# Staggered start addresses in SBUF for the operands of a hybrid attention and retention layer

## The chip, the cores and the metric

The kernel runs on one NeuronCore of a Trainium2 chip. The metric is device time in microseconds. Before the change the median of three runs is 953.46 us (952.16 to 954.02). The profiled execution shown below took 951.88 us, of which 950.1 us lie between its first and its last instruction.

## The reference

One encoder layer over x of 512 rows and 2,048 columns, in float32, then a final RMSNorm:

```
mod = silu(c) @ w_ada + b_ada;  shift, scale, gate = split(mod, 3)
h    = rms_norm(x, g) * (1 + scale) + shift
proj = h @ w_in                                # 512 x 2048 times 2048 x 7168
q_a, k_a, v_a, z_a, q_r, k_r, v_r, z_r = split(proj)
y_a  = dilated window attention, 8 heads of 128: three patterns mixed by their log-sum-exp
y_r  = retention, 4 heads (qk 128, v 256), forward and backward, normalised per head
y    = concat(y_a * silu(z_a), y_r * silu(z_r))
out  = rms_norm(x + gate * (y @ w_out), final_gain)
```

## The kernel before

TensorE multiplies float32 data in its reduced form (float32r). To keep float32 accuracy each operand is split in a high part, which is the value rounded to that form, and a low part, which is what the rounding left. A product is then three matmuls, high times high (line 90) and the two mixed ones (line 92), all added up in one PSUM bank:

```
def mm3(o, lh, ll, rh, rl, start, stop, swap=False):
    nc.tensor.matmul(o, lh, rh, start=start, stop=False, skip_group_check=True)
    for a, b in ((ll, rh), (lh, rl)) if swap else ((lh, rl), (ll, rh)):
        nc.tensor.matmul(o, a, b, ...)
```

The first operand of a matmul is the stationary one, 128 x 128, which a weight load brings into the array; the second is the moving one, 256 or 512 columns. In the profile's rows "pp<-wlo,hh" the moving operand stands first.

**Tiles.** h is held transposed, as 16 tiles hh0 to hh15 of its high parts (line 98), each 128 partitions by 512 floats, and as low parts hl in six groups (line 200). A row of 512 floats is 2,048 bytes in a partition. Weights come from HBM into tiles called raw (line 78), 1,024 floats long. conv (line 167) turns 512 of them into a pair: ScalarE copies to whi (line 174), VectorE subtracts to get wlo (line 179). There are three buffers of each. In the first part a unit of 256 columns of the projection has either "T" form, where weights are stationary and h moves with 512 columns, or "N" form, where h is stationary and 256 columns of weights move (line 647).

**Stages.** The prelude (lines 95 to 477) loads x and c, turns x with TensorE and makes the shift and scale of the first row block; its pools xp, x3p and aap are given back when it is done. While x is turned, a few matmuls of constant tiles, ident and ones, are issued to keep TensorE going (warm, line 399). Then h is made in chunks of 1, 2, 2, 3, 4 and 4 row blocks, and for every chunk the first 13 projection units (of 28) get their share of products; VectorE adds these up in SBUF (acc, line 955; in the rows, "pw" is the bank of such a share and "pp" the bank of a whole unit). The other units run over all 16 blocks at once (whole, line 1058). Attention heads (line 743) and retention heads (line 806) are cut in pieces that stand in a queue, and after every block of matmuls one group of pieces is taken from it (run_queue, line 591). Matmuls of attention and retention show as sp, tp and op.

**Output projection.** y is split like h: yh and yl, 16 tiles each, from pool opA (lines 1163 to 1171), in the place that h had. Three passes take 512, 512 and 512 columns with weights moving ("po", whi and wlo; line 1123), a fourth takes 256, and the last 256 columns are split earlier and kept in tiles lhi and llo of pool yp (line 1270). finish (line 1216) adds the residual and takes squares, and store (line 1241) scales and writes out.

**Order.** Everything is issued in the order of the Python code; in the prelude pin keeps that order. Loads run ahead of their conversion by LEAD or LEAD1 items and conversions ahead of their matmuls by LOOK items (feed, line 600). Nearly all loads are issued by SyncE's queue.

**Pools.** const (line 56) holds constants to the end: among them c_row (line 95), bg_row (line 112), ones (line 138) and row0 (line 314). wp holds raw, whi and wlo. hp holds hh and hl. The left pools are stacked from low addresses up, hp and opA from the high end down.

Of the kernel before, what the change touches and what calls it, by code (L numbers as in the profile page):

```python
# [9 lines left out]
F32 = mybir.dt.float32  # L10
F32R = mybir.dt.float32r
# [6 lines left out]
P = 128  # L18
D = 2048
S = 512  # L20
NT = S // P
NK = D // P
# [18 lines left out]
FIRST_W = OFF_KA + UC  # L41
LAG = 3
RAW, RAW1, WB, LOOK, LEAD, LEAD1, EB, YB = 3, 3, 3, 2, 4, 8, 1, 22
GR = 2
GATE_RATE = 0.9
N_FIRST = 13
# [4 lines left out]
def trunk_kernel(ctx, tc, x, c, norm_gain, w_ada, b_ada, w_in, w_out, dec_f, dec_b, final_gain, out):  # L51
    nc = tc.nc
# [3 lines left out]
    const = ctx.enter_context(tc.tile_pool(name="const", bufs=1))  # L56
    wp = ctx.enter_context(tc.tile_pool(name="wp", bufs=2))
# [5 lines left out]
    def bank(pool, nm):  # L63
        return pool.tile([P, 512], F32, tag="b", name=nm)
# [7 lines left out]
    def f32(ap):  # L72
        return ap.bitcast(F32)
# [18 lines left out]
            nc.tensor.matmul(o, a, b, start=False, stop=stop and b is (rl if swap else rh), skip_group_check=True)  # L92


    c_row = const.tile([NK, P], F32, name="c_row")
    hp_scope = ExitStack()
    hp = hp_scope.enter_context(tc.tile_pool(name="hp", bufs=1, side="right"))
    hh = [hp.tile([P, S], F32R, name=f"hh{k}") for k in range(NK)]

    groups = [range(sum(CHUNKS[:i]), sum(CHUNKS[: i + 1])) for i in range(len(CHUNKS))]  # L100
    xt_tiles = {i: hp.tile([P, len(g), S], F32, tag=f"g{i}", name=f"xT{i}") for i, g in enumerate(groups) if i}
# [6 lines left out]
    xp = x_scope.enter_context(tc.tile_pool(name="xp", bufs=1, side="right"))  # L108

    bg_row = const.tile([48, P], F32, name="bg_row")
    raw0 = [xp.tile([P, NK, P], F32, name=f"raw0{b}") for b in range(2)]
    xn = [(x3p if t == 3 else xp).tile([P, D], F32, name=f"xt{t}") for t in range(NT)]

# [19 lines left out]

    ident = const.tile([P, P], F32, name="ident")
    make_identity(nc, ident)
    ones = const.tile([P, P], F32, name="ones")
    nc.gpsimd.memset(ones, 1.0)
    ones_r = const.tile([P, 1], F32R, name="ones_r")  # L140
    mhalf = const.tile([P, 4], F32, name="mhalf")
# [14 lines left out]
    pin = tc.keep_in_program_order  # L156
    marks = {}

    def after(ins, ref):
        tc.add_manual_dep(  # L160
            ins.ins,
            ref.ins.name,
            mybir.DependencyInfo(mybir.DependencyClass.NoSync, mybir.DependencyReason.DATA),
            reason="after",
        )

    def conv(src, n, pin_low=None):
        hi = wp.tile([P, 512], F32R, tag="whi", name="whi", bufs=WB)
        lo = wp.tile([P, 512], F32R, tag="wlo", name="wlo", bufs=WB)
        dh, dl = hi[:, :n], lo[:, :n]  # L170
        if len(src.shape) == 3:
            dh = dh.rearrange("p (k f) -> p k f", k=src.shape[1])
            dl = dl.rearrange("p (k f) -> p k f", k=src.shape[1])
        c1 = nc.scalar.copy(dh, src)  # L174
        if pin_low is not None:
            pin_low.append(lambda: pin(nc.vector.tensor_tensor(dl, src, f32(dh), op=ALU.subtract)))
            pin(c1)
            return hi, lo
        c2 = nc.vector.tensor_tensor(dl, src, f32(dh), op=ALU.subtract)  # L179
        marks["conv"] = marks.get("conv", 0) + 1  # L180
        if marks["conv"] < 3:
            after(c1, marks["hh"])
            after(c2, marks["hl"])
        return hi, lo
# [126 lines left out]
    psk3 = bank(psM, "psk3")  # L311


    row0 = const.tile([1, 2 * P], F32, name="row0")

    def sums0(b, i):
        for a in range(8 * i, 8 * i + 8):
# [80 lines left out]

    def warm(n, ps):
        for _ in range(n):  # L400
            pin(nc.tensor.matmul(ps[:, 128:256], ones, ident, start=True, stop=True))

    A, B = slice(0, 3 * P), slice(3 * P, S)
    warm(WARM[0], psk3)
    squares_a(0)
    squares(0)
# [3 lines left out]
    scaled(0, P, 1024)  # L410
    silu_c()
    warm(WARM[1], psk3)
    k0_part(0)
    turned(0, 0)
# [6 lines left out]
    for t in (1, 2):  # L421
        squares_a(t)
        squares(t)
        factor(t)
    warm(WARM[2], psk3)
    turn_rows()
    sums0(0, 0)
# [18 lines left out]
    sums0_turned()  # L446
    pinned = []
    first_w = conv(raw_w[:, : 2 * UC], 2 * UC, pinned)
    shift_scale0()
    turned(1, 2)  # L450
# [108 lines left out]
    def shared_conv(c0s, k0, nk):  # L559
# [16 lines left out]
        def cv(j):  # L576
            off = (c0s[j] - lo_c) // UC
            if nk == 1:
                if k0 == 0 and lo_c == FIRST_W:
                    st[0] = first_w  # L580
                if off // 2 not in st:
                    a, b = off // 2 * 512, min(off // 2 * 512 + 512, m * UC)
                    st[off // 2] = conv(st["raw"][:, 0, a:b], b - a)
                w = st[off // 2]
                o = off % 2 * UC
                return w[0][:, o : o + UC], w[1][:, o : o + UC]
            return conv(st["raw"][:, :, off * UC : (off + 1) * UC], nk * UC)
# [336 lines left out]
    for ci, nk in enumerate(CHUNKS):  # L924
# [18 lines left out]
        for u in order:  # L943
# [22 lines left out]
            if u < N_PERSIST:  # L966
                pss = lambda u=u: persist[u]
                start, stop = ci == 0, lastc
            elif u in kept:
                pss = lambda u=u, kept=kept: kept[u]  # L970
                start, stop = False, u not in keep_now
            else:
                pss = lambda: [bank(psA, "pw") for _ in range(2)]
                start, stop = True, u not in keep_now
# [19 lines left out]
    def gate_pieces(h):  # L994
        st = {}
        gs = slice(2 * D + h * 512, 2 * D + (h + 1) * 512)

        def load(kr):
            raws[h * NK + kr] = pools["w"].tile([P, 512], F32, tag="graw", name="graw", bufs=GR)
            nc.sync.dma_start(raws[h * NK + kr], wa[kr * P : (kr + 1) * P, gs])  # L1000

        def add(kr):
            raw = raws[h * NK + kr]
            if kr == 0:
                st["acc"] = pools["w"].tile([P, 512], F32, tag="gacc", name="gacc", bufs=1)
                nc.vector.tensor_scalar_mul(st["acc"], raw, ct[:, 0:1])
            else:
                nc.vector.scalar_tensor_tensor(  # L1008
                    st["acc"], raw, ct[:, kr : kr + 1], st["acc"], op0=ALU.mult, op1=ALU.add
                )  # L1010

        def parts():
            st["parts"] = conv(st["acc"], 512)

        def total():
            row = pools["w"].tile([1, 512], F32, tag="grow", name="grow", bufs=1)
            nc.sync.dma_start(row, b_ada[0:1, gs])
            ps = bank4("psg")[0:1, :]
            for i in range(2):
                nc.tensor.matmul(ps, ones_r, st["parts"][i], start=i == 0, stop=i == 1)  # L1020
            nc.vector.tensor_tensor(row, row, ps, op=ALU.add)
            nc.sync.dma_start(grow_d[0:1, h * 512 : (h + 1) * 512], row)

        return load, add, parts, total
# [6 lines left out]
    gp = [gate_pieces(h) for h in range(4)]  # L1031
    for n in range(4 * NK + GR):

        def step(n=n):
            if n >= GR:
                gp[(n - GR) // NK][1]((n - GR) % NK)
            if n < 4 * NK:
                gp[n // NK][0](n % NK)

        gate.append(step)  # L1040
        if n >= GR and (n - GR) % NK == NK - 1:
            gate.extend([None, gp[(n - GR) // NK][2], gp[(n - GR) // NK][3]])
    gcount = [0]
# [114 lines left out]
    yh, yl = [y0[:, 0:S].bitcast(F32R)], [y0[:, S : 2 * S].bitcast(F32R)]  # L1158
# [3 lines left out]

    opA = ctx.enter_context(tc.tile_pool(name="opA", bufs=1, side="right"))
    for k in range(NK):
        hi = opA.tile([P, S], F32R, name=f"yh{k}")
        lo = opA.tile([P, S], F32R, name=f"yl{k}")
        if k:
            yh.append(hi)
            yl.append(lo)
        else:  # L1170
            y0 = hi, lo
# [135 lines left out]
    for t in range(NT):  # L1307
        ts = slice(t * P, (t + 1) * P)
        ps = bank(psP, "po")[:, :256]
# [30 lines left out]
```

## Time and profile before

| what | value |
|---|---|
| runs, median (lowest to highest) | 953.46 us (952.16 to 954.02) |
| profiled execution, its span | 951.88 us, 950.1 us |
| granted TensorE clock, mean | 0.997 |
| instructions of TensorE | 5,602 matmuls, 5,602 weight loads |
| moved by DMA | 141.50 MB, 149 GB/s on average |

A row of a table of groups gives the source line, engine, operation, tile written and tiles read, shapes and count; then the busy time in us and the mean duration of one in ns; then the idle time of the engine just before these instructions and what ended it. A row of the timeline gives start and length in us, engine, line, operation and tiles. Successive matmuls overlap in time, so the distance between the starts of two of them is shorter than the duration of one.

### The profile page before, as it was taken

What the parts mean: (1) busy time and instruction counts of PE and PEld (TensorE: products, weight loads), DVE (VectorE), ACT (ScalarE), POOL (GpSimd) and SP (SyncE); (2) the same over time, 40 slices, a digit from 0 to 9 for tenths busy, and PEclk for the clock granted to TensorE, in tenths of its full rate; (3) what the DMA queues carried; (4) which work ended last, traced back from release to release, by engine and by line L of the source; (5) the groups of instructions that cost most, each with busy time, mean ns of one, the idle gap of its engine ahead of it and who ended that gap; (6) DMA issues with size and microseconds to landing.
All of it is one profiled execution on the core that took longest, in us unless ns stands there. A gap on an engine that the chain in (4) does not pass through costs nothing.

```text
span 950.1 us, 14445 instructions
## 1 busy us (share of the span) xinstructions
PE 928.7 (98%) x5602; PEld 812.3 (85%) x5602; DVE 619.6 (65%) x1096; ACT 379.0 (40%) x747; POOL 12.5 (1%) x25
## 2 busy tenths in 40 slices
PE   7899999999999999999999999999999999999996
PEld 5787788888888888988998899998899978888896
DVE  4899999959787876765456555746734283455543
ACT  4842425252254655544344232432333362333321
POOL 1000000000000000000000000000000000000000
PEclk9999999999999999999999999999999999999998
DMA  9997898533642222212225616436322267334304
GB/s 328 337 310 244 267 327 292 163 94 121 206 149 70 87 67 67 63 50 89 68 67 178 199 45 211 127 98 209 112 67 90 67 199 257 98 111 133 111 1 178
DMA packets 110244, 141.50 MB, mean 149 GB/s; under 512 B 5800, under 2 KB 81496, under 8 KB 109792
## 3 DMA queue, kind: packets, MB, share of 16 engines
q1 hardware_dynamic: 109072, 137.27, 45.0%
q10 hardware_dynamic: 1008, 3.28, 0.9%
q8 instruction: 44, 0.72, 0.3%
q14 instruction: 24, 0.20, 0.1%
q0 software_dynamic: 96, 0.03, 0.0%
HBM read 136.36 MB, written 4.20 MB: 148 GB/s over the span
## 4 chain that ended last, share of the span: by engine, by line
PE 81%; DVE 6%; DMA 6%; ACT 2%; issue 2%; SPq 1%; POOL 0%; POOLq 0%; DVEq 0%; ACTq 0%
PE pp L92 23%; PE po L92 12%; PE pp L90 12%; PE pw L92 12%; PE po L90 6%; PE pw L90 6%; PE op L92 3%; DMA graw<-in_w_ada_dram 2%; DMA araw<-in_w_ada_dram 2%; PE sp L92 2%; PE op L90 2%; PE tp L783 1%; DVE wlo L179 1%; DVE aacc L235 1%; SPq L117 1%
## 5 line engine op out<-in xcount | busy, mean ns | idle before, releaser
L174 ACT CAST whi<-raw 128x512 fp32r<-128x512 f32 (+1 forms) x289 | 174.8, 606 | 402.6 <-PE pp L92 186.5
L179 DVE TENSOR_TENSOR wlo<-raw,whi 128x512 fp32r<-128x512 f32 (+1 forms) x288 | 193.0, 671 | 185.4 <-ACT whi L174 181.1
L92 PE MATMUL pp<-wlo,hh 128*128 128x256 f32 x576 | 160.4, 278 | 0.5 <-DVE wlo L179 0.5
L90 PE MATMUL pp<-whi,hh 128*128 128x256 f32 x576 | 160.8, 279 | 0.0
L92 PE MATMUL pp<-whi,hl 128*128 128x256 f32 x576 | 160.1, 278 | 0.0
L92 PEld LDWEIGHTS pp<-wlo,hh 128*128 128x128 f32 x576 | 108.2, 188 | 1.6 <-DVE wlo L179 0.7
L90 PEld LDWEIGHTS pp<-whi,hh 128*128 128x128 f32 x576 | 108.3, 188 | 1.1 <-issue 0.2
L92 PEld LDWEIGHTS pp<-whi,hl 128*128 128x128 f32 x576 | 108.7, 189 | 0.0
L90 PE MATMUL pw<-hh,whi 128*128 128x512 f32 x256 | 102.4, 400 | 4.7 <-ACT acc L953 2.6
L90 PE MATMUL pp<-hh,whi 128*128 128x512 f32 x256 | 101.0, 394 | 0.4 <-DVE kl L683 0.4
L92 PE MATMUL pw<-hh,wlo 128*128 128x512 f32 x256 | 100.7, 394 | 0.1
L92 PE MATMUL pp<-hl,whi 128*128 128x512 f32 x256 | 100.8, 394 | 0.0
L92 PE MATMUL pp<-hh,wlo 128*128 128x512 f32 x256 | 100.7, 395 | 0.0
L92 PE MATMUL pw<-hl,whi 128*128 128x512 f32 x256 | 100.2, 391 | 0.0
L92 PE MATMUL po<-wlo,yh 128*128 128x512 f32 (+1 forms) x252 | 92.5, 367 | 0.0
L92 PE MATMUL po<-whi,yl 128*128 128x512 f32 (+1 forms) x252 | 92.4, 367 | 0.0
L90 PE MATMUL po<-whi,yh 128*128 128x512 f32 (+1 forms) x252 | 92.4, 367 | 0.0
L235 DVE SCALAR_TENSOR_TENSOR aacc<-araw,ct,aacc 128x512 f32<-128x512 f32 (+2 forms) x75 | 76.0, 1013 | 5.5 <-ACT aacc L231 4.3
L955 DVE TENSOR_TENSOR acc<-acc,pw 128x512 f32<-128x512 f32 x100 | 66.8, 682 | 7.3 <-PE pw L92 7.1
L1008 DVE SCALAR_TENSOR_TENSOR gacc<-graw,ct,gacc 128x512 f32<-128x512 f32 x60 | 44.9, 749 | 39.2 <-DMA graw<-in_w_ada_dram 38.5
L90 PEld LDWEIGHTS pw<-hh,whi 128*128 128x128 f32 x256 | 48.1, 188 | 20.0 <-DVE acc L955 5.7
L90 PEld LDWEIGHTS pp<-hh,whi 128*128 128x128 f32 x256 | 48.2, 188 | 11.2 <-DVE kl L683 0.9
(241 smaller groups left out, 1565.1 us busy)
## 6 DMA issues: line engine op xcount, KB each, us to landing
raw<-in_w_in_dram SPq DMA_DIRECT2D x94, 512.0 KB, 3.8
araw<-in_w_ada_dram SPq DMA_DIRECT2D x48, 512.0 KB, 5.8
graw<-in_w_ada_dram SPq DMA_DIRECT2D x64, 256.0 KB, 3.0
raw<-in_w_out_dram SPq DMA_DIRECT2D x32, 512.0 KB, 4.0
raw<-in_w_in_dram SPq DMA_DIRECT2D x16, 384.0 KB, 5.1
araw<-in_w_ada_dram SPq DMA_DIRECT2D x16, 384.0 KB, 4.9
res<-in_x_dram SPq DMA_DIRECT2D x16, 256.0 KB, 6.5
raw<-in_w_in_dram SPq DMA_DIRECT2D x11, 256.0 KB, 5.8
```

Source lines behind the costliest of these rows:

```text
L90: nc.tensor.matmul(o, lh, rh, start=start, stop=False, skip_group_check=True)
L92: nc.tensor.matmul(o, a, b, start=False, stop=stop and b is (rl if swap else rh), skip_group_check=True)
L117: q.dma_start(raw0[b][:, i * 8 : (i + 1) * 8], wa[i * 8 * P : (i + 1) * 8 * P, b * D : b * D + P].rearrange("(a p) f -> p a f", p=P),)
L174: c1 = nc.scalar.copy(dh, src)
L179: c2 = nc.vector.tensor_tensor(dl, src, f32(dh), op=ALU.subtract)
L235: ins = nc.vector.scalar_tensor_tensor(acc[:, :, :n], rv[:, a], ct[:, kr + a : kr + a + 1], acc[:, :, :n], op0=ALU.mult, op1=ALU.add,)
L783: nc.tensor.transpose(tp_[:, j * P : (j + 1) * P], pt[:, j * P : (j + 1) * P], ident)
L955: nc.vector.tensor_tensor(accs[u][i], accs[u][i], ps[i], op=ALU.add)
L1008: nc.vector.scalar_tensor_tensor(st["acc"], raw, ct[:, kr : kr + 1], st["acc"], op0=ALU.mult, op1=ALU.add)
```

## The change

Tiles of hh and of yh get 24 floats (PAD) more than they use, so that the next tile begins 2,144 bytes on instead of 2,048; within its tile the data begin at float 0 for k = 0 to 3 and 8 to 11 and at float 4 for the others. whi and wlo get the same PAD; whi begins at float 0 and wlo at float 4. The low parts hl and yl stay as they are. To make room, c_row, bg_row and row0 are allocated from the prelude's pool xp instead of const, and ones has one column instead of 128; the warm-up matmuls take ident as stationary operand in place of ones.

```diff
+PAD = 24
-    c_row = const.tile([NK, P], F32, name="c_row")
+    def stagger(k):
+        return k // 4 % 2 * 4
...
-    hh = [hp.tile([P, S], F32R, name=f"hh{k}") for k in range(NK)]
+    hh = [hp.tile([P, S + PAD], F32R, name=f"hh{k}")[:, stagger(k) : stagger(k) + S] for k in range(NK)]
...
-    bg_row = const.tile([48, P], F32, name="bg_row")
+    c_row = xp.tile([NK, P], F32, name="c_row")
+    bg_row = xp.tile([48, P], F32, name="bg_row")
...
-    ones = const.tile([P, P], F32, name="ones")
+    ones = const.tile([P, 1], F32, name="ones")
...
-        hi = wp.tile([P, 512], F32R, tag="whi", name="whi", bufs=WB)
-        lo = wp.tile([P, 512], F32R, tag="wlo", name="wlo", bufs=WB)
+        hi = wp.tile([P, 512 + PAD], F32R, tag="whi", name="whi", bufs=WB)[:, 0:512]
+        lo = wp.tile([P, 512 + PAD], F32R, tag="wlo", name="wlo", bufs=WB)[:, 4:516]
...
-    row0 = const.tile([1, 2 * P], F32, name="row0")
+    row0 = xp.tile([1, 2 * P], F32, name="row0")
...
-            pin(nc.tensor.matmul(ps[:, 128:256], ones, ident, start=True, stop=True))
+            pin(nc.tensor.matmul(ps[:, 128:256], ident, ident, start=True, stop=True))
...
-        hi = opA.tile([P, S], F32R, name=f"yh{k}")
+        hi = opA.tile([P, S + PAD], F32R, name=f"yh{k}")[:, stagger(k) : stagger(k) + S]
         lo = opA.tile([P, S], F32R, name=f"yl{k}")
```

## The prediction

> **What bounds the kernel now.** I read the page first: its span, the engines' shares, the clock and the chain that ended last.
>
> ```profile
> span 950.1 us, 14445 instructions
> ...
> PE 928.7 (98%) x5602; PEld 812.3 (85%) x5602; DVE 619.6 (65%) x1096; ACT 379.0 (40%) x747; POOL 12.5 (1%) x25
> ...
> PEclk9999999999999999999999999999999999999998
> ...
> PE 81%; DVE 6%; DMA 6%; ACT 2%; issue 2%; SPq 1%; POOL 0%; POOLq 0%; DVEq 0%; ACTq 0%
> ```
>
> TensorE is busy 928.7 of 950.1 us at the full granted clock, and 81% of the chain is its own work. So the time is the number of matmuls times the distance between their starts, and every nanosecond of that distance counts. The table by stage says where this does not hold (columns: stretch, its length, then busy time and count of PE, PEld, DVE, ACT, POOL, then clock, DMA share, GB/s).
>
> ```profile
> 65.00:115.00 50.00, 47.52 (x202) 35.76 (x201) 49.18 (x77) 21.46 (x49) 0.00 (x0) 1.00 0.81 262
> ...
> 250.00:570.00 320.00, 319.48 (x1909) 280.25 (x1908) 208.08 (x390) 142.99 (x269) 1.02 (x1) 1.00 0.31 97
> 570.00:760.00 190.00, 189.41 (x1404) 178.52 (x1403) 100.17 (x156) 65.78 (x125) 3.03 (x3) 1.00 0.39 123
> 760.00:895.00 135.00, 134.61 (x583) 108.20 (x582) 70.78 (x121) 50.20 (x95) 0.00 (x0) 1.00 0.47 152
> ```
>
> From 250 us on PE leaves less than 1 us of each stretch free. Only between 65 and 115 us is VectorE the fuller engine (49.18 of 50 us).
>
> The change adds and removes no matmul, so I looked for what sets the distance between two starts. The timeline gives starts; here are the first and the last matmul of five undisturbed runs.
>
> ```profile
> 696.75 0.28 PE L92 MATMUL pp<-wlo,hh 128*128 128x256 f32 x1
> ...
> 704.91 0.28 PE L92 MATMUL pp<-wlo,hh 128*128 128x256 f32 x1
> ```
> ```profile
> 572.74 0.28 PE L90 MATMUL pp<-whi,hh 128*128 128x256 f32 x1
> ...
> 582.99 0.28 PE L90 MATMUL pp<-whi,hh 128*128 128x256 f32 x1
> ```
> ```profile
> 654.66 0.39 PE L92 MATMUL pp<-hl,whi 128*128 128x512 f32 x1
> ...
> 667.93 0.39 PE L90 MATMUL pp<-hh,whi 128*128 128x512 f32 x1
> ```
> ```profile
> 799.69 0.39 PE L92 MATMUL po<-wlo,yh 128*128 128x512 f32 x1
> ...
> 822.79 0.40 PE L92 MATMUL po<-wlo,yh 128*128 128x512 f32 x1
> ```
> ```profile
> 919.75 0.28 PE L90 MATMUL po<-lhi,yh 128*128 128x256 f32 x1
> ...
> 929.95 0.28 PE L92 MATMUL po<-llo,yh 128*128 128x256 f32 x1
> ```
>
> They hold 73, 88, 59, 100 and 86 matmuls. One step is 8.16/72 = 113.3 ns, 10.25/87 = 117.8, 13.27/58 = 228.8, 23.10/99 = 233.3 and 10.20/85 = 120.0 ns. The first two runs are the same instruction with the same shapes and tiles: the same code runs at 113.3 for a while and at 117.8 for a while, and 120.0 has 256 columns too. So there are lasting paces, a quick one and slower ones. The steps also lie on a grid: 113.3, 120.0 and 233.3 are 17, 18 and 35 times 6.67 ns; 117.8 and 228.8 are 53 and 103 times a third of it, that is, three products (high·high and the two mixed ones) take whole multiples together. [...]
>
> The groups by form show how often each pace holds. The duration of a matmul in the trace is its step plus about 163 ns:
>
> ```profile
> L92 PE MATMUL pp<-wlo,hh 128*128 128x256 f32 x28 | 7.7, 276 | 0.0
> ```
> ```profile
> L92 PE MATMUL pp<-wlo,hh 128*128 128x256 f32 x72 | 20.2, 281 | 0.0
> ```
>
> is the same group in the first run (276, step 113.3) and around the second (281, step 117.8). Over the whole span:
>
> ```profile
> L90 PE MATMUL pp<-whi,hh 128*128 128x256 f32 x576 | 160.8, 279 | 0.0
> ...
> L90 PE MATMUL pw<-hh,whi 128*128 128x512 f32 x256 | 102.4, 400 | 4.7 <-ACT acc L953 2.6 <-DVE acc L955 1.8
> ...
> L92 PE MATMUL pw<-hl,whi 128*128 128x512 f32 x256 | 100.2, 391 | 0.0
> L92 PE MATMUL po<-wlo,yh 128*128 128x512 f32 x188 | 74.5, 396 | 0.0
> ...
> L92 PE MATMUL pw<-wlo,hh 128*128 128x256 f32 x192 | 53.1, 277 | 0.0
> L92 PE MATMUL po<-llo,yh 128*128 128x256 f32 x64 | 18.1, 283 | 0.0
> ...
> L92 PE MATMUL po<-whi,yl 128*128 128x256 f32 x64 | 18.0, 281 | 0.0
> ...
> L92 PE MATMUL op<-vx,pth 128*128 128x256 f32 x32 | 9.0, 280 | 0.0
> ```
>
> The projections with 256 columns stand at 277 to 279, some 40% of the way from 276 to 281. The output projection with 512 columns stands at 396 throughout, which is 233.3 + 163: it never has the quick pace. The retention products and the last two passes (280, 281, 283) do not have it either.
>
> **The change part by part.** *Staggering.* Before, every tile of hh, whi, wlo and yh is 2,048 bytes long in a partition, so within a pool all of them begin at one place modulo 2,048. By the allocator's addresses of the program before, whi begins at byte 39,840, hh0 at 163,808 and yh at the same place modulo 2,048 as hh: all 32 bytes past a multiple of 64. The tiles of yp, which hold lhi and llo, begin at a multiple of 64; with them as moving operand against yh the step is 120.0, the worst of the three seen with 256 columns. That says the relative place matters, not only chance. With PAD = 24 a tile is 2,144 bytes, so successive tiles begin 96 bytes apart modulo 128; stagger() adds 16 bytes for every second four, and wlo begins 16 bytes later. The pool wp as a whole begins lower by what leaves const (512, 512, 1,024 and 508 bytes a partition). hl and yl stay. A matmul and its next weight load then stand in a relation that changes from k to k and between high and low, and no single pace can hold for 10 us as in the runs above.
>
> What it is worth is bounded by the paces. If all matmuls took the quickest lasting one: projections, 256 columns, 2,304 at about 278 - 276 = 2 ns, 4.6 us. Projections, 512 columns, 1,536: the group means run from 391 to 400, and the dear end holds waits (4.7 us idle before it). Against 228.8 + 163 = 391.8, taking 394.5 in the middle, 4.2 us. Output with 512 columns, 576 at 233.3 - 228.8, 2.6 us. The two last passes, 192 at 281 - 276 and 192 at 283 - 276 (the dearest row of that pass), 1.0 and 1.3 us. Retention products, 192 at 280 - 276, 0.8 us. Sum 14.5 us at most from paces that the trace shows.
>
> On the other side, if the projections took the worst paces seen: 2,304 at 120.0 - 115 (278 - 163) are 11.5 us, and 1,536 at 233.3 - 231.5 (394.5 - 163) are 2.8 us, 14.3 us more, with the rest as it is. An offset of 16 bytes is in no row, so a step under 113.3 is neither excluded nor priced here. I take 8 us of the 14.5: a mixture over all relations leaves some products in the dear one, but the output stage and the last passes, 5.7 us of the sum with the retention products, can hardly get worse, because they are at dear paces the whole time.
>
> The trace says 117.8 against 113.3 for one instruction. [...]
>
> *Writers of the moved tiles.* ScalarE writes whi and hh, VectorE reads whi and writes wlo:
>
> ```profile
> L174 ACT CAST whi<-raw 128x512 fp32r<-128x512 f32 (+1 forms) x289 | 174.8, 606 | 402.6 <-PE pp L92 186.5
> L179 DVE TENSOR_TENSOR wlo<-raw,whi 128x512 fp32r<-128x512 f32 (+1 forms) x288 | 193.0, 671 | 185.4 <-ACT whi L174 181.1
> ```
> ```profile
> L179 DVE TENSOR_TENSOR wlo<-raw,whi 128x512 fp32r<-128x512 f32 x17 | 11.6, 684 | 0.0
> ```
> ```profile
> L179 DVE TENSOR_TENSOR wlo<-raw,whi x288: 415/686/696, 31.2 to 911.1; 128x512 fp32r<-128x512 f32 x140, 128x256 fp32r<-128x256 f32 x4
> ```
>
> The third row is the group between 65 and 115 us, the fourth its shortest, median and longest. All of them read and write contiguous floats before and after; I cost the offset at nothing. Cover: ScalarE waits 402.6 us ahead of whi, most of it on PE, and VectorE has room outside that stretch. Without cover are the 17 of the stretch: at the longest duration seen, 696 for 684 ns, they cost 0.2 us; with 25 ns each (696 - 671) 0.4 us. A gain is bounded the same way, 0.4 us. In that stretch a quicker PE gains nothing, as VectorE is the fuller engine: its 202 matmuls take 0.4 us out of the 8, which is inside the rounding.
>
> *Prelude.* c_row, bg_row and row0 move to the prelude's pool, ones shrinks to one column, and the warm-up multiplies ident by itself.
>
> ```profile
> 2.08 0.22 POOL L139 MEMSET ones<- 128x128 f32 x1
> ...
> 2.61 0.11 POOL L144 MEMSET mln<- 128x1 f32 x1
> ...
> 2.69 4.20 PE L401 MATMUL psk<-ident,ones 128*128 128x128 f32 x22 [2.69 <-POOL mln L144]
> ```
>
> The memset falls from 0.22 to about the 0.11 of a column, and whatever is queued behind it on POOL (two DMA issues of bg_row) comes 0.1 us earlier. The warm-up starts at most 0.1 us earlier; the x rows that PE needs next arrive later anyway. The same DMAs go out on the same queues. Tiles that later take the pool's bytes now also wait for the last reader of row0, PE's turn of it, which happens before the turns of x that they wait for already. Zero, and 0.1 us either way if I misjudge that.
>
> Sum: -8 us from the staggering, 0 from the rest. Against the profiled execution (951.88 us, 950.1 of them span) this is 943.9; the median shown is 953.46, 1.6 us higher, so I forecast 945.5.
>
> **The rivals.** *Out of step more often.* The present layout may be the good one: 32 against 32 bytes is the only relation in which 113.3 occurs, and lhi against yh, half a grid apart, gives 120.0. Staggering takes the projections out of that relation for most k. Place: lines 90 and 92 under pp and pw, 3,840 matmuls, so that each nanosecond of their mean step costs 3.8 us. Full price 14.3 us; with half of the products at the dear pace 7 us, 960.5. It decides from the point where the projections' mean rises by more than the output and retention products can give back: 5.7/3.84 = 1.5 ns. For it speaks the 120.0; against it that the slow 117.8 arises in the old relation too, and lasts.
>
> *No effect.* The paces may be set by when a run starts, since both come with the same addresses; new addresses then only reshuffle which run falls into which. Time 953.5 give or take 1.9 us. [...]
>
> *The writers become slow.* 0.4 us by the bound above, too little to decide.
>
> **How the numbers follow.** Quicker steps 0.53, no effect 0.17, out of step 0.30. The forecast is the first case, 945.5 us; its own range is 936 (all of the 14.5 us and 3 for steps under 113.3) to 951.5. The 8-in-10 range goes on into the dear case to 960.5 and is 936 to 960.5. A difference under 0.2%, 1.9 us, can hardly be told from none; the three cases are divided at that mark.
>
> **What would show it.** Right: the group means of pp and pw with 256 columns at 276 or less, and of po with 512 columns well under 396, with no long run at one step of 117.8. Wrong: pp and pw at 281 or more (out of step), or all means as before (no effect), or the whi and wlo groups longer than 606 and 671 with more idle time ahead of PE.

## The result and the profile after

The changed kernel takes 961.4 us (median of four runs, 960.49 to 963.37) against 953.52 us (952.16 to 954.02) for the kernel before: 1.0088 times as long, with a 95% interval of 1.0068 to 1.0107. The change makes the kernel slower, where the prediction had it quicker by 8 us, and the median lies 0.9 us above the upper end of the range. The profiled execution took 963.37 us, the longest of the four; that of before, 951.88 us, is near the short end of its runs. Between the two profiles there are thus 11.5 us, of which 7.9 are the difference of the medians.

The page of the profile after, its span, the engines' shares, the chain, and the two groups of writers:

```profile
span 961.6 us, 14452 instructions
...
PE 940.1 (98%) x5602; PEld 821.4 (85%) x5602; DVE 619.8 (64%) x1096; ACT 379.0 (39%) x747; POOL 13.4 (1%) x25
...
PE 82%; DVE 6%; DMA 6%; issue 2%; SPq 1%; ACT 1%; POOLq 0%; POOL 0%; DVEq 0%; ACTq 0%
...
L179 ACT CAST whi<-raw 128x512 fp32r<-128x512 f32 (+1 forms) x289 | 174.6, 606 | 410.6 <-PE pp L93 188.1
L184 DVE TENSOR_TENSOR wlo<-raw,whi 128x512 fp32r<-128x512 f32 (+1 forms) x288 | 193.1, 671 | 189.1 <-ACT whi L179 183.8
```

PE's busy time went from 928.7 to 940.1 us, 11.4 us for the same 5,602 matmuls, and the span grew by 11.5. Everything else stayed: VectorE and ScalarE are as busy as before, and the writers of the moved tiles take 606 and 671 ns as they did. The whole loss is in the distance between matmuls. The groups by form show where (the step is the duration less about 163 ns):

```profile
L91 PE MATMUL pp<-whi,hh 128*128 128x256 f32 x576 | 162.5, 282 | 0.0
L93 PE MATMUL pp<-wlo,hh 128*128 128x256 f32 x576 | 162.0, 281 | 0.7 <-DVE wlo L184 0.7
...
L93 PE MATMUL pw<-hl,whi 128*128 128x512 f32 x256 | 101.5, 397 | 0.0
...
L93 PE MATMUL po<-wlo,yh 128*128 128x512 f32 x188 | 74.4, 396 | 0.0
L93 PE MATMUL po<-whi,yl 128*128 128x512 f32 x188 | 74.2, 395 | 0.0
...
L93 PE MATMUL po<-llo,yh 128*128 128x256 f32 x64 | 18.0, 281 | 0.0
```

Projections with 256 columns went from 278 or 279 to 281 or 282, the one with hl from 391 to 397; the output stage fell by up to one (396 to 395), the last pass from 283 to 281. Taking all starts of the two traces, step by step:

| matmuls | count | before, us | after, us | mean step before and after, ns |
|---|---|---|---|---|
| projection, 256 columns | 2,304 | 268.2 | 275.8 | 114.85, 118.21 |
| projection, 512 columns | 1,536 | 365.0 | 370.2 | 229.91, 232.10 |
| output, 512 columns | 576 | 135.3 | 134.3 | 233.28, 232.29 |
| output, lhi and llo | 192 | 22.9 | 22.6 | 119.98, 118.46 |

(The mean steps leave out the gaps with a wait in them, the totals do not.) The sum is 7.6 + 5.2 - 1.0 - 0.3 = 11.5 us. The spell of 96 matmuls that held the prediction's first run, at 113.3 ns, begins and ends like this in the timeline of after:

```profile
706.28 0.28 PE L91 MATMUL pp<-whi,hh 128*128 128x256 f32 x1
...
717.55 0.28 PE L93 MATMUL pp<-whi,hl 128*128 128x256 f32 x1
```

That is 11.27/95 = 118.6 ns, with steps between 113 and 125 ns that change from k to k. Staggering did what the prediction said it does, no pace lasts any more. But the mixture is dearer than what it replaces.

### The profile page after: what moved, and what is told of

Same layout as the page of the kernel before. It is cut to its first block, busy times and chain, and to the rows that moved or that the text cites. A ratio compares the mean times of both kernels' runs of the same rounds, so it can differ in the third digit from the quotient of the medians.

```text
span 961.6 us, 14452 instructions
## 1 busy us (share of the span) xinstructions
PE 940.1 (98%) x5602; PEld 821.4 (85%) x5602; DVE 619.8 (64%) x1096; ACT 379.0 (39%) x747; POOL 13.4 (1%) x25
## 4 chain that ended last, share of the span: by engine, by line
PE 82%; DVE 6%; DMA 6%; issue 2%; SPq 1%; ACT 1%; POOLq 0%; POOL 0%; DVEq 0%; ACTq 0%
PE pp L93 23%; PE pw L93 13%; PE po L93 12%; PE pp L91 12%; PE pw L91 6%; PE po L91 6%; PE op L93 3%; DMA araw<-in_w_ada_dram 3%; DMA graw<-in_w_ada_dram 2%; DVE aacc L240 2%; PE sp L93 2%; PE op L91 2%; DVE wlo L184 1%; PE tp L788 1%; DVE acc L960 1%
## 5 line engine op out<-in xcount | busy, mean ns | idle before, releaser
L93 PEld LDWEIGHTS pw<-hh,wlo 128*128 128x128 f32 x256 | 48.4, 189 | 12.3 <-DVE wlo L184 1.4
```

## The experiments

In the trace of before, the weight load of the next matmul starts about 3 ns after a matmul (the median over all of them) and takes 188 ns on the mean of the row below, less than the 276 ns and more of a matmul with 256 columns. So the load of the next stationary operand lies inside the matmul ahead of it.

```profile
L92 PEld LDWEIGHTS pp<-wlo,hh 128*128 128x128 f32 x576 | 108.2, 188 | 1.6 <-DVE wlo L179 0.7
```

I write **d** for the start of the next stationary operand less the start of the moving one, in bytes of a partition, modulo 256. By the allocator's addresses, before has whi and wlo at 160 and hh, hl, yh and yl at 224 modulo 256. So N units and the output passes have d = 64, T units d = 192. (A matmul's own stationary operand begins at the same place modulo 256 as the next one, here and in the blocks of m2, so the runs do not tell which of the two counts.) The expectations name these theories: A, one place of an operand lets the quick pace last; B, the relation of the pair does, modulo 64; C, the edits of the prelude cost the time; D and E, the relation of the pair modulo 128 and modulo 256.

**The parts of the change.** e1_prelude_only keeps the edits of the prelude and undoes all padding:

```diff
-    hh = [hp.tile([P, S + PAD], F32R, name=f"hh{k}")[:, stagger(k) : stagger(k) + S] for k in range(NK)]
+    hh = [hp.tile([P, S], F32R, name=f"hh{k}") for k in range(NK)]
...
-        hi = wp.tile([P, 512 + PAD], F32R, tag="whi", name="whi", bufs=WB)[:, 0:512]
-        lo = wp.tile([P, 512 + PAD], F32R, tag="wlo", name="wlo", bufs=WB)[:, 4:516]
+        hi = wp.tile([P, 512], F32R, tag="whi", name="whi", bufs=WB)
+        lo = wp.tile([P, 512], F32R, tag="wlo", name="wlo", bufs=WB)
...
-        hi = opA.tile([P, S + PAD], F32R, name=f"yh{k}")[:, stagger(k) : stagger(k) + S]
+        hi = opA.tile([P, S], F32R, name=f"yh{k}")
```

> The edits of the prelude alone, no padding and no offsets; as a side effect whi and wlo begin at a multiple of 64 bytes while hh, hl, yh and yl begin 32 bytes past one, and lhi and llo now begin 32 past one too. Theory A (a single place for each operand lets a quick pace last; mixed places do not): projections with 256 columns keep a lasting pace, group means 277 to 279 ns as before, time 952 to 955 us. Theory B (each pair pays by its own relation, 32 bytes apart is the dear one): projections with 256 columns at 283 ns, time 962 to 966 us, and the last pass, whose operands now stand at one place, falls from 282 to 276 to 281 ns. Theory C (the prelude's edits cost the time, not the places): 961 us with the means of the matmuls as before.

e2_pad64 keeps the padding but moves all in steps of 64 bytes: PAD = 16, no offsets, and a tile of 32 bytes ahead of const that shifts the pools behind it.

> The change with PAD of 16 floats and no 16-byte offsets, and 32 bytes more in front of wp, so that hh, hl, yh, yl, whi and wlo all begin 32 bytes past a multiple of 64, as before the change, but no longer at one place modulo 128 or 2,048. Theory A and theory B: as before the change, 952 to 955 us, projections with 256 columns at 277 to 279 ns. If places modulo 128 or 2,048 are what counts, or if the prelude's edits cost the time: 958 to 962 us.

e3_w_only keeps padding and offset for whi and wlo alone, with hh and yh as before and the same 32 bytes ahead of const.

> Padding and offset of whi and wlo alone, hh, hl, yh and yl as before the change. Theory A: the moving operand of the N form changes its place from matmul to matmul, so no pace lasts, projections with 256 columns at 281 to 282 ns, those with 512 at 395 to 397, time 958 to 961 us. Theory B: half of the pairs stay at one place, so half of the loss, 956 to 958 us.

| kernel | median, us | ratio to before, 95% |
|---|---|---|
| e1_prelude_only | 962.77 | 1.0081 [1.0059, 1.0102] |
| e2_pad64 | 958.68 | 1.0049 [1.0035, 1.0064] |
| e3_w_only | 961.42 | 1.0075 [1.0060, 1.0090] |

In e2 every tile stays 32 bytes past a multiple of 64, for which theories A and B had 952 to 955 us; it takes 958.68. In e3 the stagger of whi and wlo alone costs about as much as the whole change, with steps of 118.3 ns in the N units, 231.8 in the T units and 232.9 in the output stage; that is nearer to A (958 to 961) than to B (956 to 958).

The surprise is e1: without any staggering it loses as much as the whole change. Its groups by form:

```profile
L91 PE MATMUL pp<-whi,hh 128*128 128x256 f32 x576 | 162.6, 282 | 0.0
...
L93 PE MATMUL pw<-hl,whi 128*128 128x512 f32 x256 | 101.7, 397 | 0.0
...
L93 PE MATMUL po<-wlo,yh 128*128 128x512 f32 x188 | 74.5, 396 | 0.0
```

Its tiles lie at one place modulo 2,048 again, yet its steps are 118.3 ns in the N units and 233.2 in the T units. What is left of the change is that const is 2,528 bytes shorter, so that wp, which lies behind it, moved from 160 to 192 modulo 256 while hp stayed at 224. The time is near the 961 us of theory C, but C had the means of the matmuls as before, and they rose. It also fits B as it was put (962 to 966 us, N at 283, the last pass at 276 to 281; it took 281). The edits and the places are still to be told apart.

**The law, with matmuls alone.** m1_steps and m2_places, one execution each, leave the layer out and store x; they issue blocks of 60 and 50 matmuls, twice each, with given starts of the moving operand (mv) and the stationary one (st):

```
for i in range(NMM):
    m = mo[i % len(mo)] // 4
    s = so[i % len(so)] // 4 + i % 4 * P
    pin(nc.tensor.matmul(b[:, :n], st[:, s : s + P], mv[:, m : m + n], ...))
```

> A kernel of matmuls alone that leaves the whole layer out and stores x: blocks of 60 matmuls with 256 or 512 columns, nothing else at work on the moving and stationary tiles; moving and stationary operand begin at chosen places modulo 64 bytes (a: 0 and 0; b: 0 and 16; c: 0 and 32; d: 0 and 48; e: moving 0 and 16 in turn; f: stationary 0 and 16 in turn; g: moving 0 and 32 in turn; h: all four in turn for both). Theory A: a to d each show one lasting step, 113.3 or 117.8 ns at 256 columns, whatever the relation; e to h a mean of 117 to 119 ns. Theory B: a, b and d 113.3 ns, c 120 ns, e and f 113.3 ns, g and h in between. With 512 columns 228 to 230 ns against 232 ns.

The groups by form of m1 (a: no offset; b: stationary 16 bytes on; f: stationary at 0 and 16 in turn; h: four places of each in turn):

```profile
L49 PE MATMUL b<-mv,st 128*128 128x512 f32 x120 | 28.5, 397 | 1.3 <-DVE st L62 1.3
...
L49 PE MATMUL h<-mv,st 128*128 128x512 f32 x120 | 28.2, 395 | 1.3 <-DVE st L62 1.3
...
L49 PE MATMUL a<-mv,st 128*128 128x512 f32 x120 | 27.7, 391 | 1.3 <-DVE st L62 1.3
L49 PE MATMUL f<-mv,st 128*128 128x512 f32 x120 | 27.7, 390 | 1.2 <-DVE st L62 1.2
...
L49 PE MATMUL a<-mv,st 128*128 128x256 f32 x120 | 14.9, 284 | 1.2 <-DVE st L62 1.2
...
L49 PE MATMUL h<-mv,st 128*128 128x256 f32 x120 | 14.6, 282 | 1.3 <-DVE st L62 1.3
```

The matmuls of the blocks with one number of columns differ in their start addresses alone, and their steps differ. With both at the same place a step is 226.67 ns for 512 columns, quicker than any of the five paces seen in the kernel before, and 120.0 for 256, as dear as its dearest. 16 bytes of offset cost 6.7 ns with 512 columns (233.3) and gain 1.7 with 256 (118.3); 48 bytes give 123.3. The mixture h has 117.9 and 231.5. A mixture need not come to the average of its parts: f, half at the relation of a and half at that of b, has 226.7 with 512 columns, where the average is 230.0. Theory B had 113.3 ns for a, theory A 113.3 or 117.8 for each of a to d; a took 120.0 and d 123.3, so neither holds as it was put. None had 113.3, so the good place lay beyond 48 bytes.

> Matmuls alone as in m1_steps (the layer is left out, x is stored), blocks of 50 with 256 and 512 columns, the stationary operand 0, 32, 64, 96, 128, 160, 192 and 224 bytes behind the moving one modulo 256 (a to h), then both 32 bytes on (i), and moving at 160 with stationary at 224 and the other way round (j, k: the places of whi and hh before the change). Theory D: c, g, j and k (64 apart modulo 128) take 113.3 or 117.8 ns at 256 columns, a, e and i 120.0 ns and 226.7 ns at 512; c and g alike and a and e alike if 128 is the period. Theory B (modulo 64): c like a. If the period is longer than 128, a and e or c and g differ.

The groups by form of m2 (a: d = 0, c: 64, e: 128, g: 192, k: 192 too, with the moving operand at 224):

```profile
L53 PE MATMUL c<-mv,st 128*128 128x512 f32 x100 | 23.7, 396 | 0.0
...
L53 PE MATMUL e<-mv,st 128*128 128x512 f32 x100 | 23.6, 395 | 0.0
...
L53 PE MATMUL g<-mv,st 128*128 128x512 f32 x100 | 23.2, 392 | 0.0
L53 PE MATMUL a<-mv,st 128*128 128x512 f32 x100 | 23.2, 391 | 1.3 <-DVE st L67 1.3
...
L53 PE MATMUL a<-mv,st 128*128 128x256 f32 x100 | 12.5, 285 | 1.2 <-DVE st L67 1.2
...
L53 PE MATMUL e<-mv,st 128*128 128x256 f32 x100 | 12.2, 281 | 0.0
...
L53 PE MATMUL g<-mv,st 128*128 128x256 f32 x100 | 12.1, 279 | 0.0
...
L53 PE MATMUL c<-mv,st 128*128 128x256 f32 x100 | 11.7, 276 | 0.0
...
L53 PE MATMUL k<-mv,st 128*128 128x256 f32 x100 | 11.7, 276 | 0.0
```

Between the starts in the second half of each block, the same in both turns:

| d, bytes | 0 | 32 | 64 | 96 | 128 | 160 | 192 | 224 |
|---|---|---|---|---|---|---|---|---|
| 256 columns, ns | 120.0 | 118.3 | 113.3 | 120.0 | 118.5 | 120.0 | 117.8 or 113.3 | 116.7 |
| 512 columns, ns | 226.7 | 233.3 | 233.3 | 234.2 | 232.6 | 233.3 | 228.9 | 233.3 |

a against e and c against g differ, so the period is longer than 128 bytes (theory D falls, and B, in which c was like a); 256 fits all that was run. Pairs at other places with the same d (i: moving and stationary both at 32, group means 283 and 389 ns; j: 160 against 224, 276 and 396) have the paces of d = 0 and d = 64 in the second half of the block, so it is the relation that counts, not one place (A falls). The table gives the kernels back. Before: at d = 64 N should have 113.3 and the output stage 233.3, T at 192 228.9 (its mean is 229.9), and the lhi and llo pass, at 160, 120.0; those are four of the five paces of the prediction, and the fifth, 117.8, comes with m3 below. e1: N at d = 32 118.3, the output stage there 233.3, T at 224 233.3. After spreads over all the places and others between them: the mean over the eight columns (with 117.8 for 192) is 118.1 and 232.0 ns, and after has 118.2 and 232.1 to 232.3. e2 visits the four columns that are multiples of 64, whose means are 117.4 and 230.4; it has 117.9 and 231.3 to 232.0. Why d = 192 shows two paces with 256 columns was not followed up by itself; e5 below has both of them too, and m3 shows the same for d = 64.

**The law, in the kernel.** e4_same128 and e5_apart64 are e1 with 32 and 96 bytes ahead of const, which give N d = 0 and d = 192:

```diff
+    const.tile([P, 8], F32, name="fill")
```

> The edits of the prelude, no padding and no offsets, and 32 bytes in front of all constants: whi and wlo begin at the same place modulo 128 as hh, hl, yh and yl (before the change they begin 64 bytes apart from them). Theory D (the place of the moving against the stationary operand modulo 128 bytes decides which paces can last; the blocks of m1_steps with both at one place had 120.0 ns at 256 columns and 226.7 ns at 512): projections with 256 columns at 283 ns, with 512 columns at 390 ns, the output projection with 512 columns at 390 ns instead of 396, time 955 to 958 us. Theory C (the prelude's edits cost 7 to 8 us): 960 to 963 us.

> The same with 96 bytes in front instead of 32, so that all tiles stand 64 bytes apart modulo 128 exactly as before the change, while ident, ones, c_row, bg_row and row0 stand as in the change. Theory D: the paces of before, projections with 256 columns at 277 to 279 ns, time 952 to 955 us. Theory C: 960 to 963 us.

```profile
L92 PE MATMUL pp<-whi,hh 128*128 128x256 f32 x576 | 163.9, 284 | 0.0
...
L94 PE MATMUL pw<-hl,whi 128*128 128x512 f32 x256 | 100.2, 391 | 0.0
...
L94 PE MATMUL po<-wlo,yh 128*128 128x512 f32 x188 | 73.4, 390 | 0.0
```

These are e4's groups: steps of 119.8 in N, 228.0 in T and 226.9 in the output stage, as the table says for d = 0, up to 1.3 ns in T. It takes 955.73 us, 1.0030 [1.0016, 1.0043]. One pass does not fit: by the same addresses lhi and llo stand at d = 96, where the table has 120.0, and their mean step is 117.4 (in e1, at 128, it is 118.6, and in e5, at 32, 118.3, both within 0.1 of the table). Whether d = 96 has a second pace was not run. The groups of e5 are these:

```profile
L92 PE MATMUL pp<-whi,hh 128*128 128x256 f32 x576 | 161.5, 280 | 0.0
...
L94 PE MATMUL pw<-hl,whi 128*128 128x512 f32 x256 | 101.2, 395 | 0.0
...
L92 PE MATMUL po<-whi,yh 128*128 128x256 f32 x64 | 17.7, 276 | 0.0
```

N stands at 117.4 on the mean, T at d = 64 at 233.35, the output stage at 228.9 with 512 columns and, for the first time in that pass, at 113.3 with 256. So N and that pass have the two paces of d = 192 in one kernel. Time 958.62 us, 1.0059 [1.0041, 1.0077], where theory D had 952 to 955: modulo 128 it fails in the kernel too. Between e1 and e4, 32 bytes of fill move N by 1.5, T by 5.2 and the output stage by 6.4 ns a matmul, each to about the value of its column.

**Shift and stagger apart.** e6_as_before is e1 with 224 bytes ahead of const, which brings back d = 64; e7_stagger_only is the whole change with the same 224 bytes.

> The edits of the prelude, no padding and no offsets, and 224 bytes in front of all constants, so that whi and wlo begin 64 bytes before hh, hl, yh and yl modulo 256, as before the change. Theory E (the place of the next stationary operand behind the moving one, modulo 256 bytes, sets the paces; the blocks of m2_places gave 113.3 ns at 64 with 256 columns, 228.9 at 192 and 233.3 at 64 with 512 columns): the paces of before, projections with 256 columns at 277 to 279 ns, output projection with 512 columns at 396, time 952 to 955 us. Theory C (the prelude's edits cost the time): 958 to 963 us.

> The whole change with the same 224 bytes in front of all constants, so that the pool of whi and wlo begins where it would without padding 64 bytes before hh modulo 256; the padding and the 16-byte offsets stay. Theory E: the operands meet in many relations modulo 256, most of them at 117 to 120 ns and 231 to 234 ns, so the staggering costs on its own what the change cost, 959 to 963 us. Rival (the shift of the pool by the bytes taken from const is the whole cost, staggering costs nothing): 952 to 955 us.

One group with 256 columns and one with 512 of e6, then of e7:

```profile
L92 PE MATMUL pp<-whi,hh 128*128 128x256 f32 x576 | 160.9, 279 | 0.0
...
L94 PE MATMUL po<-wlo,yh 128*128 128x512 f32 x188 | 74.5, 396 | 0.0
```
```profile
L92 PE MATMUL pp<-whi,hh 128*128 128x256 f32 x576 | 162.3, 282 | 0.0
...
L94 PE MATMUL po<-wlo,yh 128*128 128x512 f32 x188 | 74.3, 395 | 0.0
```

e6 takes 952.18 us, 0.9990 [0.9979, 1.0002]: with the old relation restored nothing remains of e1's 8 us, so neither the moved rows nor the smaller ones nor the new warm-up costs anything that these runs show (C falls as a mechanism). Its steps are those of before: 115.09 ns in N, 229.63 in T, 233.28 in the output stage with 512 columns. wp stands 2,304 bytes, nine times 256, below its old place, which changes no relation modulo 256 but every one modulo 512, and the paces are the old ones; so nothing here asks for a period of 512. e7 takes 959.84 us, 1.0078 [1.0060, 1.0096], with steps of 118.15, 231.39 and 232.33 ns: the stagger costs about 7 us without the shift too. The two costs do not add up; each by itself takes the projections from a good relation, one to a worse one, the other to about the average of all.

**A kernel placed by the table.** e8_placed is e6 with whi and wlo at two places, so that N keeps d = 64 while T units and the 512-column output passes get d = 0; lhi and llo are shifted to d = 64.

```diff
-    def conv(src, n, pin_low=None):
-        hi = wp.tile([P, 512 + PAD], F32R, tag="whi", name="whi", bufs=WB)[:, 0:512]
-        lo = wp.tile([P, 512 + PAD], F32R, tag="wlo", name="wlo", bufs=WB)[:, 4:516]
+    def conv(src, n, pin_low=None, o=16):
+        hi = wp.tile([P, 576], F32R, tag="whi", name="whi", bufs=WB)[:, o : o + 512]
+        lo = wp.tile([P, 576], F32R, tag="wlo", name="wlo", bufs=WB)[:, o : o + 512]
...
+                    o=0 if mode == "N" else 16,
...
+                    o=0 if n == 256 else 16,
```

> No staggering; every operand is put at the relation that was quickest in m2_places: 64 bytes modulo 256 where weights move with 256 columns, 0 where 512 columns move (whi and wlo are filled 64 bytes later for those units and for the output projection), and lhi and llo 64 before yh. Theory E: projections with 512 columns at 226.7 + 163 = 390 ns instead of 394, output projection with 512 columns 390 instead of 396, the last pass 276 instead of 282; gain 1,536 x 2.4 + 576 x 6.6 + 192 x 6.7 ns = 3.7 + 3.8 + 1.3 us, time 943 to 947 us. If the relation of single operands in the blocks does not carry over to the kernel: 951 to 956 us.

It takes 949.08 us, 0.9964 [0.9950, 0.9978], the shortest of all, 4.3 us under before on the same chip, but short of the 943 to 947 us that were expected. Its groups:

```profile
L92 PE MATMUL pp<-whi,hh 128*128 128x256 f32 x576 | 161.6, 281 | 0.0
...
L92 PE MATMUL pw<-hh,whi 128*128 128x512 f32 x256 | 102.7, 401 | 5.6 <-DVE acc L966 2.7 <-ACT acc L964 2.1 <-ACT whi L180 0.5
...
L94 PE MATMUL pp<-hl,whi 128*128 128x512 f32 x256 | 99.9, 390 | 0.0
...
L94 PE MATMUL po<-wlo,yh 128*128 128x512 f32 x188 | 73.3, 390 | 0.0
```

T and the output stage went to 227.8 and 226.8 ns as placed; the lhi and llo pass went from 120.0 to 117.8, not to the 113.3 that was expected. The profiled execution of e8 took 950.93 us, the longest of its six runs, so the two traces lie only 1 us apart. In them two things took part of the gain that was expected. N rose from 114.85 to 116.41 although its d is the old one, 3.8 us by the totals of the two traces. And the gaps with waits among the T matmuls grew from 11.9 to 15.0 us: in the first part PE waits for the sums of VectorE and ScalarE, as the row with 5.6 us of idle time shows (4.7 before). That this comes of the quicker matmuls is not shown: e4, whose T units are as quick, has 12.3 us of such gaps, and e6, whose T units run as in before, 13.1.

The first of these was the 113.3 and 117.8 of the prediction again: of the 768 groups of three products in the N units 489 were within 1 ns of 113.3 and 220 within 1 ns of 117.8 a step in before, 229 and 503 in e8. A spell, which is a run of N matmuls with no others between, settles on one of the two in its first few matmuls and keeps it; of the 44 spells of 18 and more matmuls one in each trace changed it, behind a gap with a wait. m3_entry is m2 with only d = 64 and 256 columns, and with a few other matmuls straight ahead of each block.

> Matmuls alone: the layer is left out and x is stored as the output. Twelve blocks, two turns, of 50 matmuls with 256 columns, all at the places of the kernel before (moving operand 160, next stationary operand 224 modulo 256, d = 64). Ahead of a block, with no gap, stand other matmuls: none (a); six, seven or eight with 512 columns at d = 64 (b, c, d), six or seven at d = 0 (e, f), six or seven at d = 192 (g, h), six at d = 32 (i), six with 256 columns at d = 0 or 32 (j, k), six with 128 columns (l). Theory F: at d = 64 both paces, 113.3 and 117.8 ns, hold for as long as nothing disturbs them, and what stands just ahead of a spell settles which one it is. Then blocks that differ only in what stands ahead of them divide into some at 113.3 and some at 117.8 ns (group means 276 and 281 ns), each block the same in both turns. Rival: the pace is a matter of what ScalarE, VectorE and the transfers do at the same time, or of the tile's absolute place. Then nothing disturbs these blocks and all twelve go to 113.3 ns (276 ns) after a few matmuls.

Groups by form (b, c and d: six, seven and eight matmuls of 512 columns at d = 64 ahead; g and h: six and seven at d = 192):

```profile
L52 PE MATMUL c<-mv,st 128*128 128x256 f32 x100 | 12.1, 281 | 0.0
...
L52 PE MATMUL h<-mv,st 128*128 128x256 f32 x100 | 12.1, 281 | 0.0
...
L52 PE MATMUL g<-mv,st 128*128 128x256 f32 x100 | 11.7, 276 | 0.0
L52 PE MATMUL d<-mv,st 128*128 128x256 f32 x100 | 11.7, 276 | 0.0
L52 PE MATMUL b<-mv,st 128*128 128x256 f32 x100 | 11.7, 276 | 0.0
```

Six blocks go to 113.33 ns and six to 117.8, each the same in both turns. One matmul more ahead of the block turns one into the other (b, c, d: group means of 276, 281 and 276 ns). So at d = 64 either pace can last for a whole block, the code and the addresses of the block being the same, and what runs straight ahead of it settles which one. That is the likeliest account of the slow spells of e8: its N spells are as before, but the T matmuls ahead of them run at another pace. By the starts of the two traces, the eight spells straight behind T matmuls all settle at 113.3 in before and all at 117.8 in e8, where T has d = 0; in m3, too, the blocks behind matmuls at d = 0 with 512 columns (e and f) go to 117.8. Of the 14 spells behind score matmuls (sp) all are quick in before and ten slow in e8. How to enter always at the quick one was not tried.

## Why the prediction was wrong

**Right.** That the time is the number of matmuls times their distance (11.4 of the 11.5 us between the two profiles are PE's busy time), that lasting paces set that distance, that the relation of the two operands counts, and that staggering ends the lasting paces. The grid holds in part: 113.3, 120.0, 226.7 and 233.3 are whole multiples of 6.67 ns, but m2 also has lasting paces, such as 116.7 and 118.3, that are neither that nor whole multiples of a third of it. The writers cost nothing (606 and 671 ns, as before). The output stage and the last pass did get quicker, by 1.0 and 0.3 us.

**The step that failed first** is "I take 8 us of the 14.5: a mixture over all relations leaves some products in the dear one, but the output stage and the last passes ... can hardly get worse". It sets the mixture between the present state and the quickest pace. In the changed kernel the mixture came to about the average of all relations, which the table puts at 118.1 and 232.0 ns; it measured 118.21 and, in T, 232.10. The projections were on the good side of it, at 114.85 and 229.9, and they are 3,840 of the matmuls; only the output stage, 768, was on the bad side. The trace of before could have warned: all its five paces came from three relations, and the average over others was in no row. I took the paces seen for a fair sample.

**The second failed step** is "all 32 bytes past a multiple of 64". The relation counts modulo 256, where whi and hh are 64 apart. Reading both as the same place hid that T and N units, the same pair with roles exchanged, stand in two different relations (192 and 64), and that the output stage with 512 columns, at 233.3, stands in the one in which N has its quick pace. So one relation can be good for 256 columns and dear for 512 (113.3 and 233.3 at d = 64 in m2).

**The third** is "Zero" for the prelude. The instructions do cost nothing (e6), but the bytes that leave const move wp by 32 modulo 256, and that alone is worth 8 us (e1). I had written that wp "begins lower by what leaves const" and drew nothing from it. In the changed kernel this comes on top of a stagger that spreads the relation anyway, so the loss stays at 8 us instead of doubling. A smaller slip is "hl and yl stay": yl lies between the yh tiles in one pool, so its starts move by 96 bytes from k to k. The 3 us for steps under 113.3, in the lower end of the range, come from no row, and no run shows such a lasting step: the quickest with 256 columns is 113.3 in m2 and m3 too.

**The rival "out of step more often"** has the right cause, the relation of the operands, and the right size: half of the products at the dear pace was priced at 7 us and 960.5; the medians are 7.9 us apart. It also gave the point from which it decides, a rise of the projections' mean by 1.5 ns; the rise was 3.4 and 2.2. The rival "no effect" is refuted by e1 and e6 (962.77 and 952.18 us, the same edits with wp 224 bytes apart), and in m2 matmuls of 256 columns that differ in the start of the stationary operand alone take 113.3 ns a step at d = 64 and 120.0 at d = 0. One half of that rival holds: at d = 64 the same addresses have two paces, 113.3 and 117.8 ns, and the way into a block chooses (m3).

That the relation sets the pace is shown by m2 with the matmuls alone and by e1, e4, e5 and e6 in the kernel. Why it does, and why 256 bytes fit as its period, no run here shows; starts off the 32-byte grid were measured by themselves only in m1 (16 and 48 bytes), and only products in float32r were measured.

## What to carry to other kernels

Before spreading addresses, measure what each relation of moving and next stationary operand costs: here spreading gave about the average of all, 118.2 ns in the projections with 256 columns, which loses wherever the present place is better than that, as 114.85 was. An edit that changes the bytes of a pool can move the pools behind it (here 2,528 bytes less in const moved wp, and the time rose by 8 us in e1), so compare the start addresses of the operands, modulo 256 bytes here, before putting a difference down to the edit itself. Where the pace of identical instructions comes in two lasting values, look at what stands just ahead of each spell.

## What the runs showed of the hardware

With one matmul after the other in float32r, each with its own weight load, the lasting step for 256 columns lay between 113.3 ns (m2, d = 64) and 123.3 (m1, 48 bytes) and for 512 between 226.7 (m2, d = 0) and 234.2 (m2, d = 96), set by the difference of two start addresses modulo 256 bytes and, at d = 64 with 256 columns, by what ran just ahead as well (113.3 or 117.8, m3), at a granted clock of 1.00 in these three runs. No one relation of those that were run is best for both: d = 0 has the quickest 512 and a slow 256 columns (226.7 and 120.0), d = 64 the reverse (233.3 and 113.3). The quickest steps, 113.3 and 226.7, are 17 and 34 times 6.67 ns.
